# Expert outputs kept one row per choice, and the last two experts' rows brought to the tokens by one-hot matmuls

## The chip, the cores and the metric

The kernel runs on one core of one Trainium2 chip. The metric is the device time of one execution in microseconds (us), and the median of several runs is compared. The engines are named in the profile as PE (TensorE matmuls) with PEld (its weight loads), DVE (VectorE), ACT (ScalarE), POOL (GpSimd) and SP (SyncE, which issues most DMAs). A name with a q behind it (SPq, POOLq) is the engine's sequencer, which issues DMAs, waits and branches. Tiles are 128 partitions wide; S and D, the tokens and the model's width, are both 1024, so that a [1024, 1024] tensor in f32 has 4.19 MB.

## The reference

One decoder layer: attention of two kinds side by side, a cross-attention into memory tokens, a mixture of experts, a final RMS norm. The change touches the mixture's output and the norm:

```python
# each token: one group of experts, then the top 2 experts in it, with weights
weights = (g_gate * e_gate).reshape(-1)
expert_ids = (g_sel * EXPERTS_PER_GROUP + e_sel).reshape(-1)
...
def block_fn(args):
    tok, wt, e = args
    xb = h_pad[tok]
    hidden = jax.nn.silu(xb @ w_gate[e]) * (xb @ w_up[e])
    return (hidden @ w_down[e]) * wt[:, None].astype(hf.dtype)
...
out = jnp.zeros((n_tok + 1, d), hf.dtype).at[slot_token].add(y.reshape(n_slots, d))[:n_tok]
...
x = x + _hierarchical_moe(...)
return _rms_norm(x, norm_final_g)
```

There are 32 experts; 1024 tokens with two choices each make 2048 rows of expert output, 64 to an expert on average.

## The kernel before

Most of the kernel is written against a recorder, `Sched`. An engine call is recorded, and `flush` (line 337) puts all recorded operations into a static order by a greedy simulation with its own prices, then emits them to the engines' queues in that order. An operation recorded earlier has precedence among those that are ready. `hold` and `drop` keep a tile's buffer beyond its last recorded use. In the profile nearly all operations carry the helper's line, L523, so they are told apart by the names of their tiles. SBUF tiles of 4 KB a partition come from one pool of 50 buffers (`t4`, line 588).

Up to about 842 us the kernel computes attention, cross-attention and routing. For each 128 tokens `r_keep` (line 1476) writes the normed rows to XN and the residual rows to ACC, both in DRAM. `r_index` (1603) makes `sidx`, for each of 32 experts and 96 slots the number 2 x token + choice of the row in that slot (a large number where the slot is empty), and from it `gidx`, the token.

`experts` (1762) goes over the 32 experts. For expert e, `moe_load` asks for weights up to two experts ahead, as six buffers of 0.52 MB. `m_x` gathers the expert's tokens from XN with an indirect DMA on GpSimd, `m_split` splits each weight buffer into a high and a low part (ScalarE casts, VectorE subtracts), `m_gu` and `m_h` compute the hidden layer, and `m_d` (1746) the output: two PSUM banks of 512 columns, scaled by the routing weight on ScalarE into y, then an indirect DMA on GpSimd that adds the rows to ACC. Each scatter waits for the one before, as both touch ACC.

Behind the experts the recorded operations are flushed. Then stands a block (1880 to 1998) that a register decides: where an expert has over 96 rows, it works off the rest in a loop with its own weight loads on SP and scatters on GpSimd. In the profiled execution no instruction of the block's inside ran. The block's branch is line 1881.

The tail (2002 to 2018) is recorded anew: it loads the final gain and the eight tiles of ACC, and for groups of tiles (`TAIL`) squares them on ScalarE with a sum, takes the inverse root in a chain of twelve small VectorE operations, scales on VectorE and writes out.

Of the kernel before, what the change touches and what calls it, by code (L numbers as in the profile page):

```python
# [22 lines left out]
P = 128  # L23
# [32 lines left out]
WHOLE_GU = range(0)  # L56
WHOLE_D = range(4)
WHOLE_PV = ()
TAIL = ((0,), (1, 2), (3, 4), (5, 6, 7))
PARK = range(8)  # L60
NPRE = 0
NXG = 3
# [463 lines left out]
def f32(t):  # L526
    return t.bitcast(F32)
# [30 lines left out]
def hybrid_kernel(ctx: ExitStack, tc: tile.TileContext, a, out):  # L558
# [111 lines left out]
    VD = dram.tile([NT, P, 8 * P], F32, name="VD")  # L670
    VM = dram.tile([NT, P, 8 * P], F32, name="VM")
    XN = dram.tile([S, D], F32, name="XN")
    ACC = dram.tile([S, D], F32, name="ACC")

    def rsqrt(dst, v, tmp):

# [520 lines left out]
    w3 = keep.tile([P, 3, 2, NT], BF16, name="w3")  # L1197
    wsl = keep.tile([P, NE], F32, name="wsl")
    gidx = keep.tile([P, NE], I32, name="gidx")
    w_out, w_mq, w_mo, w_mkv = (a[n].rearrange("o d c -> (o d) c") for n in  # L1200
                                ("w_out", "w_mem_q", "w_mem_o", "w_mem_kv"))
    pr = sm
# [273 lines left out]
    def r_keep(t):  # L1476

        x = t4("xn")

        nc.gpsimd.tensor_mul(x.rearrange("p (k q) -> p q k", k=KT), *[  # L1480
            v.rearrange("p (q k) -> p q k", k=KT) for v in (xr[t], rt["gb"])])
        nc.scalar.activation(x, x, AF.Copy, scale=rs_[t])
        nc.sync.dma_start(XN[t * P:(t + 1) * P], x)
        nc.sync.dma_start(ACC[t * P:(t + 1) * P], xr[t])

    def r_factors(c, *sizes):

# [115 lines left out]
    def r_index():  # L1603

        tb = acc()[0:NS, 0:NE]
        n = 0
        for c in range(NCH):
            oh, vv = lane[c]
            for k in range(2):
                for t in range(TPC):  # L1610
                    for i in range(2):
                        mm(tb, oh[:, k, t], vv[:, k, t, i * NE:(i + 1) * NE], start=n == 0, stop=n == 31)
                        n += 1
        ti = rper(NE)[0:NS]
        sidx = rper(NE, dt=I32)
        with nc.chain():
            nc.vector.tensor_scalar(ti, tb, 0.0, 4096.0, op0=OP.is_equal, op1=OP.mult)
            nc.vector.scalar_tensor_tensor(sidx[0:NS], tb, -1.0, ti, op0=OP.add, op1=OP.add)
            nc.vector.tensor_scalar(gidx[0:NS], sidx[0:NS], 1, None, op0=OP.arith_shift_right)
# [35 lines left out]
        nc.vector.tensor_copy(nov, obend[:, NE - 1:NE])  # L1655


    w_g, w_u, w_d = (a[n].rearrange("o e d f -> (o e) d f") for n in ("w_expert_gate", "w_expert_up", "w_expert_down"))
    pieces = {}

# [73 lines left out]
    def m_h(e):  # L1734
        sg = st[e]["sg"]
        hp = bank()
        for k in range(2):
            nc.tensor.transpose(hp[:, k * NS:(k + 1) * NS], sg[0:NS, k * P:(k + 1) * P], ident[0:NS, 0:NS])
        if e in WHOLE_D:
            h = st[e]["h"] = t4("hw", P, 2, CH)  # L1740
            nc.scalar.copy(h[:, 0, 0:2 * NS], hp[:, 0:2 * NS])
        else:
            h = st[e]["h"] = two("hid")
            split((h[:, 0, 0:2 * NS], h[:, 1, 0:2 * NS]), hp[:, 0:2 * NS])

    def m_d(e):
        h = st[e]["h"]
        y = t4("y")
        for n in range(2):
            yp = bank()  # L1750
            for k in range(2):
                sl = slice(k * NS, (k + 1) * NS)
                if e in WHOLE_D:
                    mm(yp[0:NS], h[:, 0, sl], pieces[e, 4 + k][:, n], start=k == 0, stop=k == 1)
                else:
                    wh, wl = st[e][4 + k]
                    mm3(yp[0:NS], h[:, 0, sl], h[:, 1, sl], wh[:, n], wl[:, n], k == 0, k == 1)
            nc.scalar.activation(y[0:NS, n * 512:(n + 1) * 512], yp[0:NS], AF.Copy, scale=wsl[0:NS, e:e + 1])
        nc.gpsimd.indirect_dma_start(out=ACC[:, :], out_offset=Rows(ap=gidx[0:NS, e:e + 1], axis=0), in_=y[0:NS],
                                     in_offset=None, bounds_check=S - 1, oob_is_err=False, compute_op=OP.add)  # L1760

    def experts():
        for e in range(NE + 1):
            if e < NE:
                for i in range(AHEAD):
                    moe_load(e + i)
                m_x(e)
                for j in range(4):
                    m_split(e, j)
                moe_load(e + AHEAD)  # L1770
                if e > 0:
                    m_h(e - 1)
                m_gu(e)
                for j in range(4, 6):
                    m_split(e, j)
            if e > 0:
                if e == NE:
                    m_h(e - 1)
                m_d(e - 1)

# [30 lines left out]
    def place(units, *knots):  # L1811

        n = len(units)
        for i, u in enumerate(units):
            x = (i + 0.5) / n * (len(knots) - 1)
            j = int(x)
            line.append((knots[j] + (x - j) * (knots[j + 1] - knots[j]), u))

    place([c_angles, u_load_q, u_load_kv], *T["ul"])
    for c in range(NCH):  # L1820
        place(c_units(c), *T[f"cu{c}"])
        place(u_units(c), *T[f"uu{c}"])
# [48 lines left out]
    nc.flush()  # L1871
    lazy, nc = nc, tc.nc
    mm = nc.tensor.matmul
    A_, obst_, obend_, rank_, nov_, hc_, w3_, XN_, ACC_ = (v.real() for v in (A, obst, obend, rank, nov, hc, w3, XN, ACC))
    ident_, iota_ = hc_[:, 32:160], hc_[:, 160:288]

    def rbank():
# [3 lines left out]
    with tc.If(rnov > 0):  # L1881
# [71 lines left out]
        with tc.For_i(0, rnov, 1) as b:  # L1953
# [37 lines left out]
            for n in range(2):  # L1991
                yp = rbank()
                for k in range(2):
                    mm(yp, hT_[:, k * P:(k + 1) * P],
                       wdn[k][:, n * 512:(n + 1) * 512], start=k == 0, stop=k == 1)
                nc.vector.tensor_scalar(y[:, n * 512:(n + 1) * 512], yp, wx, None, op0=OP.mult)
            nc.gpsimd.indirect_dma_start(out=ACC_[:, :], out_offset=bass.IndirectOffsetOnAxis(ap=ix[:, 1:2], axis=0), in_=y,
                                         in_offset=None, bounds_check=S - 1, oob_is_err=False, compute_op=OP.add)
    nc = lazy


    gf = t4("gfin")
    nc.sync.dma_start(gf, a["norm_final_g"].partition_broadcast(P))
    y_t = ACC.rearrange("(t p) d -> t p d", p=P)
    o_t = out.rearrange("o (t p) d -> (o t) p d", p=P)
    ys = [t4("yt") for _ in range(NT)]
    for t in range(NT):
        nc.sync.dma_start(ys[t], y_t[t])

    for tiles in TAIL:  # L2010
        n = len(tiles)
        ss = carve("ss1")(3, n)
        for i, t in enumerate(tiles):
            nc.scalar.activation(t4("sq"), ys[t], AF.Square, accum_out=ss[:, 0, i:i + 1])
        rsqrt_mean(ss[:, 2], ss[:, 0], D, ss[:, 1])
        for i, t in enumerate(tiles):
            nc.vector.scalar_tensor_tensor(ys[t], ys[t], ss[:, 2, i:i + 1], gf, op0=OP.mult, op1=OP.mult)
            nc.sync.dma_start(o_t[t], ys[t])


_INS = ["x", "mem", "positions", "norm_mix_g", "w_in", "diff_lambda_q1", "diff_lambda_k1", "diff_lambda_q2",
# [21 lines left out]
```

## Time and profile before

| | us |
|---|---|
| median of 3 runs | 1226.58 |
| lowest and highest run | 1223.6, 1228.83 |
| the profiled execution | 1223.93 |
| its span, first to last instruction | 1222.1 |

The profile is of one execution on the core. Busy time over the span: PE 1099.2 us, DVE 875.7, ACT 801.0, POOL 422.5. Matmuls are pipelined and their ends modelled, so PE's busy time is not its time at its peak. The clock granted to TensorE was 0.95 of full speed in the mean. The DMA share is the mean busy share of the core's 16 DMA engines.

### The profile page before, as it was taken

The numbers are of one execution on the slowest core, as the hardware profiler recorded it, in microseconds if no ns is written. First come the engines' busy times: TensorE is split into PE (matmuls) and PEld (weight loads), VectorE is DVE, ScalarE is ACT, GpSimd is POOL, SyncE is SP. The second block draws the span as 40 slices with busy tenths as digits, with TensorE's granted clock in tenths as the row PEclk, the third lists the DMA queues.
The fourth block names the chain that finished last, engine by engine and source line by source line (L and its number), as shares of the span: only waits on it lengthen the run. The fifth ranks groups of instructions, "written<-read, shape, count | busy, mean of one in ns | idle before, by whom it ended". The sixth has DMA issues, their size and how long they took to land. (4 is left out here: it accounts for less than half of the span.)

```text
span 1222.1 us, 19622 instructions
## 1 busy us (share of the span) xinstructions
PE 1099.2 (90%) x6285; PEld 897.8 (73%) x6285; DVE 875.7 (72%) x2044; ACT 801.0 (66%) x1597; POOL 422.5 (35%) x378
## 2 busy tenths in 40 slices
PE   3999999998798999999999999994998999899970
PEld 3998898897666887678999888884665776666640
DVE  5946535468899879999482466776666898778855
ACT  5735327589988789987361455651676887778853
POOL 2214321258837456966121001153132322222120
PEclk9999999999899999899899999995998999999995
DMA  9118898459844553456441132877899999999967
GB/s 299 32 49 296 306 381 254 132 156 249 214 106 134 155 159 82 121 154 201 156 139 36 36 115 70 286 230 251 274 307 284 299 307 318 324 329 331 340 206 280
DMA packets 145115, 256.56 MB, mean 210 GB/s; under 512 B 17035, under 2 KB 65522, under 8 KB 145010
## 3 DMA queue, kind: packets, MB, share of 16 engines
q1 hardware_dynamic: 128960, 208.22, 53.7%
q0 software_dynamic: 15680, 46.75, 12.7%
q8 instruction: 50, 0.82, 0.3%
q14 instruction: 55, 0.45, 0.1%
q10 hardware_dynamic: 370, 0.32, 0.1%
HBM read 208.57 MB, written 55.05 MB: 216 GB/s over the span
## 5 line engine op out<-in xcount | busy, mean ns | idle before, releaser
L523 DVE TENSOR_TENSOR elo<-eraw,ehi 128x1024 fp32r<-128x1024 f32 x182 | 218.8, 1230 | 53.8 <-ACT ehi L523 48.2
L523 ACT CAST ehi<-eraw 128x1024 fp32r<-128x1024 f32 x184 | 189.5, 1054 | 23.1 <-DMA eraw<-in_w_expert_up_dram 16.8
L523 PE MATMUL bank<-ehi,xT 128*96 128x512 f32 x512 | 173.7, 411 | 5.7 <-ACT y L523 4.3
L523 PE MATMUL bank<-k,q 128*128 128x512 f32 (+5 forms) x480 | 129.7, 379 | 8.9 <-DMA k<-KD 1.8
L523 POOL DMA_INDIRECT ACC<-y,gidx x32 | 52.3, 1633 | 216.0 <-ACT y L523 183.6
L523 DVE TENSOR_TENSOR pT<-bank,pT 128x512 fp32r<-128x512 f32 (+2 forms) x208 | 109.0, 561 | 24.0 <-ACT pT L523 23.5
L523 PE MATMUL acc<-pT,v 128*128 128x512 f32 (+3 forms) x384 | 113.2, 376 | 10.0 <-ACT pT L523 5.1
L523 PEld LDWEIGHTS bank<-ehi,xT 128*96 128x96 f32 x512 | 85.6, 167 | 43.8 <-ACT y L523 9.4
L523 ACT CAST pT<-bank 128x512 fp32r<-128x512 f32 (+2 forms) x208 | 93.4, 497 | 28.6 <-PE bank L523 27.4
L523 PE MATMUL bank<-hc,pt 128*128 128x128 f32 x640 | 102.2, 291 | 7.9 <-POOL pt L523 6.0
L523 PE MATMUL bank<-elo,xT 128*96 128x512 f32 x256 | 104.4, 408 | 1.9 <-DVE elo L523 1.4
L523 PEld LDWEIGHTS bank<-k,q 128*128 128x128 f32 (+1 forms) x480 | 82.6, 196 | 26.6 <-DVE mx L523 7.1
L523 PE MATMUL lbank<-whi,mix 128*128 128x256 f32 x512 | 97.0, 286 | 0.0
L523 PEld LDWEIGHTS bank<-hc,pt 128*128 128x128 f32 x640 | 80.8, 150 | 20.1 <-POOL pt L523 7.8
L523 PE MATMUL lbank<-whi,hT 128*128 128x256 f32 (+1 forms) x384 | 86.8, 312 | 0.0
L523 PEld LDWEIGHTS acc<-pT,v 128*128 128x128 f32 x384 | 64.8, 193 | 27.2 <-ACT pT L523 11.0
L523 PEld LDWEIGHTS lbank<-whi,mix 128*128 128x128 f32 x512 | 81.4, 192 | 0.2
L523 PE MATMUL lbank<-hT,whi 128*128 128x512 f32 x256 | 81.1, 395 | 0.0
L523 PE MATMUL bank<-ehi,hid 128*96 128x512 f32 x224 | 75.6, 395 | 1.2 <-ACT hid L523 0.8
L523 PE MATMUL lbank<-wlo,mix 128*128 128x256 f32 x256 | 72.6, 284 | 0.0
L523 DVE TENSOR_REDUCE mx<-bank 128x1 f32<-128x512 f32 (+3 forms) x112 | 61.2, 571 | 14.7 <-PE bank L523 14.4
L523 POOL TENSOR_TENSOR O<-O,sh 64x512 f32<-64x512 f32 x32 | 41.5, 1298 | 79.1 <-ACT O L523 67.0
(623 smaller groups left out, 2671.9 us busy)
## 6 DMA issues: line engine op xcount, KB each, us to landing
eraw<-in_w_expert_gate_dram SPq DMA_DIRECT2D x128, 256.0 KB
eraw<-in_w_expert_up_dram SPq DMA_DIRECT2D x128, 256.0 KB
eraw<-in_w_expert_down_dram SPq DMA_DIRECT2D x64, 512.0 KB
k<-KD SPq DMA_DIRECT2D x72, 128.0 KB
QM<-st POOLq DMA_DIRECT2D x16, 512.0 KB, 6.8
q<-QM SPq DMA_DIRECT2D x16, 512.0 KB
wraw<-in_w_out_dram SPq DMA_DIRECT2D x16, 512.0 KB
wraw<-in_w_in_dram SPq DMA_DIRECT2D x12, 512.0 KB
```

Source lines behind the costliest of these rows:

```text
L523: getattr(getattr(self.nc, eng), name)(*[real(v) for v in a], **{n: real(v) for n, v in k.items()})
```

## The change

The DRAM tensor ACC goes. Two take its place: XR, with the residual rows, and Y, with 2048 rows, one for each token's each choice. `r_keep` writes XR where it wrote ACC. Y is cleared: one tile of zeros, and 16 writes of 128 rows from it on SP, placed among the units of attention (300 to 560 us of the plan). `sidx` moves into a longer-lived tile. `m_d` scatters to Y by `sidx`, without adding. For the last two experts (`NLAST`) it doesn't scatter: it splits the two halves of y into a high part (ScalarE) and a low part (VectorE) and keeps them.

`m_end` is recorded after expert 31's gate and up products and ahead of its down product: it loads the eight tiles of XR, the sixteen tiles of Y (a tile takes the first or second choices of 128 tokens) and the final gain, and for each of the last two experts makes a one-hot matrix (slot by token) of eight pieces with 18 small VectorE operations. These loads are flushed ahead of the overflow block. The block scatters to Y and ends with its own reload of the sixteen Y tiles.

In the tail a tile is XR's plus the two of Y, plus, for each half, a PSUM bank into which four one-hot matmuls (two experts, high and low) bring the last experts' rows. The first add of even tiles, and their product with the gain, are on GpSimd; even tiles are scaled on ScalarE.

```diff
-TAIL = ((0,), (1, 2), (3, 4), (5, 6, 7))
+NLAST = 2
+TAIL = ((0, 1), (2, 3), (4, 5), (6, 7))
+TAILV = (1, 3, 5, 7)
...
-    ACC = dram.tile([S, D], F32, name="ACC")
+    XR = dram.tile([S, D], F32, name="XR")
+    Y = dram.tile([2 * S, D], F32, name="Y")
...
+    sidx = sums.rearrange("p t h -> p (t h)")[:, 0:NE].bitcast(I32)
...
-        nc.sync.dma_start(ACC[t * P:(t + 1) * P], xr[t])
+        nc.sync.dma_start(XR[t * P:(t + 1) * P], xr[t])
...
+    y_t = Y.rearrange("(t p k) d -> t k p d", p=P, k=2)
...
-            nc.scalar.activation(y[0:NS, n * 512:(n + 1) * 512], yp[0:NS], AF.Copy, scale=wsl[0:NS, e:e + 1])
-        nc.gpsimd.indirect_dma_start(out=ACC[:, :], out_offset=Rows(ap=gidx[0:NS, e:e + 1], axis=0), in_=y[0:NS],
-                                     in_offset=None, bounds_check=S - 1, oob_is_err=False, compute_op=OP.add)
+            w = wsl[0:NS, e:e + 1]
+            if e >= NE - NLAST:
+                yl = last[e, n] = two("yl")
+                nc.scalar.activation(yl[0:NS, 0], yp[0:NS], AF.Copy, scale=w)
+                nc.vector.scalar_tensor_tensor(yl[0:NS, 1], yp[0:NS], w, f32(yl[0:NS, 0]), op0=OP.mult, op1=OP.subtract)
+                nc.hold(yl)
+            else:
+                nc.scalar.activation(y[0:NS, n * 512:(n + 1) * 512], yp[0:NS], AF.Copy, scale=w)
+        if e >= NE - NLAST:
+            return
+        nc.gpsimd.indirect_dma_start(out=Y[:, :], out_offset=Rows(ap=sidx[0:NS, e:e + 1], axis=0), in_=y[0:NS],
+                                     in_offset=None, bounds_check=2 * S - 1, oob_is_err=False)
...
+    def y_zero():
+
+        z = t4("zero")
+        nc.gpsimd.memset(z, 0.0)
+        return [lambda i=i: nc.sync.dma_start(Y[i * P:(i + 1) * P], z) for i in range(2 * NT)]
+
+    def m_end():
+
+        for t in range(NT):
+            ys.append([t4("yt")])
+            nc.sync.dma_start(ys[t][0], XR[t * P:(t + 1) * P])
+        for t in range(NT):
+            for k in range(2):
+                ys[t].append(t4("yt"))
+                nc.sync.dma_start(ys[t][1 + k], y_t[t, k])
+            nc.hold(*ys[t])
+        for e in range(NE - NLAST, NE):
+            g = sm.tile([P, 1 + NT], F32, name="lastg", bufs=2)
+            nc.vector.tensor_copy(g[0:NS, 0:1], gidx[0:NS, e:e + 1])
+            oh = last[e] = t4("oh", P, NT, P, dt=F32R)
+            for t in range(NT):
+                nc.vector.tensor_scalar(g[0:NS, 1 + t:2 + t], g[0:NS, 0:1], -float(t * P), None, op0=OP.add)
+                nc.vector.tensor_scalar(oh[0:NS, t], iota_f[0:NS], g[0:NS, 1 + t:2 + t], None, op0=OP.is_equal)
+            nc.hold(oh)
+        last["gf"] = t4("gfin")
+        nc.sync.dma_start(last["gf"], a["norm_final_g"].partition_broadcast(P))
+        nc.hold(last["gf"])
...
             if e > 0:
                 if e == NE:
+                    m_end()
                     m_h(e - 1)
                 m_d(e - 1)
...
+    place(y_zero(), 300, 560)
...
+        y_t_ = Y_.rearrange("(t p k) d -> t k p d", p=P, k=2)
+        for t in range(NT):
+            for k in range(2):
+                nc.sync.dma_start(ys[t][1 + k].real(), y_t_[t, k])
     nc = lazy
...
         for i, t in enumerate(tiles):
-            nc.scalar.activation(t4("sq"), ys[t], AF.Square, accum_out=ss[:, 0, i:i + 1])
+            z, y0, y1 = ys[t]
+            (nc.vector if t in TAILV else nc.gpsimd).tensor_add(z, z, y0)
+            nc.vector.tensor_add(z, z, y1)
+            for b in range(2):
+                po = bank()
+                m = [(last[e][0:NS, t], last[e, b][0:NS, x]) for e in range(NE - NLAST, NE) for x in range(2)]
+                for x, (l, r) in enumerate(m):
+                    mm(po, l, r, start=x == 0, stop=x == len(m) - 1)
+                v = z[:, b * 512:(b + 1) * 512]
+                nc.vector.tensor_add(v, po, v)
+            nc.scalar.activation(y0, z, AF.Square, accum_out=ss[:, 0, i:i + 1])
         rsqrt_mean(ss[:, 2], ss[:, 0], D, ss[:, 1])
         for i, t in enumerate(tiles):
-            nc.vector.scalar_tensor_tensor(ys[t], ys[t], ss[:, 2, i:i + 1], gf, op0=OP.mult, op1=OP.mult)
-            nc.sync.dma_start(o_t[t], ys[t])
+            z = ys[t][0]
+            if t in TAILV:
+                nc.vector.scalar_tensor_tensor(z, z, ss[:, 2, i:i + 1], gf, op0=OP.mult, op1=OP.mult)
+            else:
+                nc.scalar.activation(z, z, AF.Copy, scale=ss[:, 2, i:i + 1])
+                nc.gpsimd.tensor_mul(z, z, gf)
+            nc.sync.dma_start(o_t[t], z)
```

## Rows read from the trace of the kernel before

**Rows 1.** Windows by stage: busy us (instructions) by engine, PEclk, DMA share, GB/s.
```profile
430.00:560.00 130.00, 122.67 (x698) 98.48 (x696) 117.72 (x342) 114.70 (x258) 87.61 (x53) 0.93 0.53 143
842.00:938.00 96.00, 83.82 (x404) 57.31 (x404) 56.87 (x69) 58.50 (x88) 26.88 (x23) 0.90 0.89 271
938.00:1024.00 86.00, 85.22 (x418) 60.40 (x417) 76.96 (x91) 74.54 (x108) 24.41 (x19) 1.00 0.99 306
1024.00:1114.00 90.00, 80.87 (x366) 54.56 (x364) 68.48 (x80) 68.44 (x96) 21.95 (x16) 0.94 1.00 329
1114.00:1176.00 62.00, 58.56 (x260) 38.37 (x259) 53.02 (x61) 52.70 (x74) 11.80 (x7) 1.00 0.99 337
1176.00:1194.00 18.00, 8.69 (x37) 5.44 (x35) 4.36 (x5) 5.58 (x9) 2.83 (x2) 0.87 0.35 71
```
**Rows 2.** Chain of waits near the end: start us, us, what.
```profile
1182.62 5.49 DMA ACC<-y,gidx
...
1188.86 5.22 DMA ACC<-y,gidx
```
**Rows 3.** Timeline, last y and last tail group: start, us, engine, operation, [idle before].
```profile
1185.64 0.69 ACT L523 ACTIVATE y<-bank,wsl 96x512 f32<-96x512 f32 x1 [0.68 <-PE bank L523]
...
1211.84 0.57 DVE L523 TENSOR_SCALAR ss<-ss 128x3 f32<-128x3 f32 x3
...
1214.22 3.68 DVE L523 SCALAR_TENSOR_TENSOR yt<-yt,ss,gfin 128x1024 f32<-128x1024 f32 x3
```
**Rows 4.** DMA queues, 850 to 1175 us: packets, MB, share; scatters, median us to land.
```profile
q1 hardware_dynamic: 38821, 84.76, 76.3%
q0 software_dynamic: 6505, 15.33, 20.0%
...
ACC<-y,gidx POOLq DMA_INDIRECT x30, 8.2
```
**Rows 5.** Groups of instructions, 850 to 1175 us: the gathers, busy us, mean ns.
```profile
L523 POOL DMA_INDIRECT xg<-XN,gidx x29 | 31.7, 1092 | 43.5 <-PE bank L523 37.1 <-issue 6.4
```
**Rows 6.** DMA queues, 840 to 870 us, GpSimd's queue with gathers alone.
```profile
q0 software_dynamic: 784, 1.89, 22.9%
...
xg<-XN,gidx POOLq DMA_INDIRECT x7, 5.9
```
**Rows 7.** DMA queues, 871 to 880 us, GpSimd's queue with one scatter.
```profile
q0 software_dynamic: 112, 0.23, 13.3%
```
**Rows 8.** The overflow block's branch on SP: duration ns, first and last start; its waits.
```profile
L1881 SPq EVENT_SEMAPHORE  x9: 17/17/17, 1170.7 to 1177.7; - x9
...
SPq L1881 <- SPq L1881: 7.3, 7, 1.9
```
**Rows 9.** Window in which the tail's loads and first writes run, columns as rows 1.
```profile
1195.50:1206.00 10.50, 0.00 (x0) 0.00 (x0) 6.36 (x27) 7.00 (x13) 0.00 (x0) 0.50 1.01 371
```
**Rows 10.** Timeline of SP's DMA issues, from the last weight pieces on.
```profile
1168.30 0.98 SPq L523 DMA_DIRECT2D eraw<-in_w_expert_down_dram  x2
1177.82 0.35 SPq L523 DMA_DIRECT2D gfin<-in_norm_final_g_dram  x1
```
**Rows 11.** Groups of VectorE by shape, whole span: busy us, mean ns, idle before.
```profile
L523 DVE TENSOR_TENSOR elo<-eraw,ehi 128x1024 fp32r<-128x1024 f32 x182 | 218.8, 1230 | 53.8 <-ACT ehi L523 48.2 <-issue 2.3 <-DMA eraw<-in_w_expert_gate_dram 1.7
L523 DVE TENSOR_TENSOR xr<-lbank,xr 128x512 f32<-128x512 f32 x16 | 11.0, 688 | 12.0 <-PE lbank L523 11.9
L523 DVE SCALAR_TENSOR_TENSOR yt<-yt,ss,gfin 128x1024 f32<-128x1024 f32 x8 | 9.9, 1282 | 0.1
```
**Rows 12.** Groups of GpSimd by shape: a product of two tiles in SBUF.
```profile
L523 POOL TENSOR_TENSOR xn<-xr,gb 128x1024 f32<-128x1024 f32 x8 | 19.3, 2414 | 53.2 <-DVE xr L523 44.4 <-ACT xn L523 5.7 <-issue 3.1
```
**Rows 13.** Timeline of GpSimd and VectorE around 833 us.
```profile
832.75 2.38 POOL L523 TENSOR_TENSOR elo<-eraw,ehi 128x1024 fp32r<-128x1024 f32 x1
833.40 1.74 DVE L523 TENSOR_TENSOR rtmp<-rtmp 128x4 f32<-128x4 f32 x1
```
**Rows 14.** DMA queues, 1183.5 to 1188.5 us, GpSimd's queue with one scatter alone.
```profile
q0 software_dynamic: 112, 0.29, 40.2%
```

More of the change, by code (lines that the diff above doesn't have):

```diff
@@ L1614, in r_index @@
         ti = rper(NE)[0:NS]
-        sidx = rper(NE, dt=I32)
         with nc.chain():
@@ L1747, in m_d @@
         h = st[e]["h"]
-        y = t4("y")
+        y = t4("y") if e < NE - NLAST else None
         for n in range(2):
@@ L1757, in m_d @@
                     mm3(yp[0:NS], h[:, 0, sl], h[:, 1, sl], wh[:, n], wl[:, n], k == 0, k == 1)
-            nc.scalar.activation(y[0:NS, n * 512:(n + 1) * 512], yp[0:NS], AF.Copy, scale=wsl[0:NS, e:e + 1])
-        nc.gpsimd.indirect_dma_start(out=ACC[:, :], out_offset=Rows(ap=gidx[0:NS, e:e + 1], axis=0), in_=y[0:NS],
-                                     in_offset=None, bounds_check=S - 1, oob_is_err=False, compute_op=OP.add)
+            w = wsl[0:NS, e:e + 1]
[10 more added lines that the diff above has]
+                                     in_offset=None, bounds_check=2 * S - 1, oob_is_err=False)
+    ys = []
+    last = {}
+    def y_zero():
[22 more added lines that the diff above has]
+        nc.hold(last["gf"])
     def experts():
@@ L1873, in hybrid_kernel @@
     mm = nc.tensor.matmul
-    A_, obst_, obend_, rank_, nov_, hc_, w3_, XN_, ACC_ = (v.real() for v in (A, obst, obend, rank, nov, hc, w3, XN, ACC))
+    A_, obst_, obend_, rank_, nov_, hc_, w3_, XN_, Y_ = (v.real() for v in (A, obst, obend, rank, nov, hc, w3, XN, Y))
     ident_, iota_ = hc_[:, 32:160], hc_[:, 160:288]
@@ L1996, in hybrid_kernel @@
                 nc.vector.tensor_scalar(y[:, n * 512:(n + 1) * 512], yp, wx, None, op0=OP.mult)
-            nc.gpsimd.indirect_dma_start(out=ACC_[:, :], out_offset=bass.IndirectOffsetOnAxis(ap=ix[:, 1:2], axis=0), in_=y,
-                                         in_offset=None, bounds_check=S - 1, oob_is_err=False, compute_op=OP.add)
+            nc.gpsimd.indirect_dma_start(out=Y_[:, :], out_offset=bass.IndirectOffsetOnAxis(ap=ix[:, 0:1], axis=0), in_=y,
+                                         in_offset=None, bounds_check=2 * S - 1, oob_is_err=False)
+        y_t_ = Y_.rearrange("(t p k) d -> t k p d", p=P, k=2)
+        for t in range(NT):
+            for k in range(2):
+                nc.sync.dma_start(ys[t][1 + k].real(), y_t_[t, k])
     nc = lazy
-    gf = t4("gfin")
-    nc.sync.dma_start(gf, a["norm_final_g"].partition_broadcast(P))
-    y_t = ACC.rearrange("(t p) d -> t p d", p=P)
+    mm = nc.tensor.matmul
+    gf = last["gf"]
     o_t = out.rearrange("o (t p) d -> (o t) p d", p=P)
-    ys = [t4("yt") for _ in range(NT)]
-    for t in range(NT):
-        nc.sync.dma_start(ys[t], y_t[t])
     for tiles in TAIL:
@@ L2013, in hybrid_kernel @@
         for i, t in enumerate(tiles):
-            nc.scalar.activation(t4("sq"), ys[t], AF.Square, accum_out=ss[:, 0, i:i + 1])
+            z, y0, y1 = ys[t]
[9 more added lines that the diff above has]
+            nc.scalar.activation(y0, z, AF.Square, accum_out=ss[:, 0, i:i + 1])
         rsqrt_mean(ss[:, 2], ss[:, 0], D, ss[:, 1])
         for i, t in enumerate(tiles):
-            nc.vector.scalar_tensor_tensor(ys[t], ys[t], ss[:, 2, i:i + 1], gf, op0=OP.mult, op1=OP.mult)
-            nc.sync.dma_start(o_t[t], ys[t])
+            z = ys[t][0]
[5 more added lines that the diff above has]
+            nc.sync.dma_start(o_t[t], z)
+    nc.drop(gf, *[v for y in ys for v in y], *[v for k, v in last.items() if k != "gf"])
 _INS = ["x", "mem", "positions", "norm_mix_g", "w_in", "diff_lambda_q1", "diff_lambda_k1", "diff_lambda_q2",
```

## The prediction

> **What bounds the kernel now.** I read first the table by stage [rows 1]. Through the expert stage (842 to 1176 us) the 16 DMA engines are full (0.89, then 0.99 to 1.00), TensorE is nearly so: 85.2 of 86 us up to 1024, then 80.9 of 90 and 58.6 of 62. So weights set the pace there, and TensorE would take over after a gain of at most its idle time, 12.2 + 0.8 + 9.1 + 3.4 = 25.5 us. From 1176 on nothing is full: the stretch to 1194 has DMA at 0.35 and TensorE at 8.7 of 18 us. The chain of waits shows what that stretch is: two accumulating scatters, one behind the other, 5.5 and 5.2 us, the second held until the first has landed [rows 2]. The last y rows are out of PSUM at 1185.64 + 0.69 = 1186.3 [rows 3], and the span ends at 1222.1: 35.8 us of tail, with VectorE's chains and scalings as its last part.
>
> **Part 1: scatters without accumulation.** Between 850 and 1175 us the queue of GpSimd's DMAs takes 20.0% of the engines, 65.0 us, for 30 scatters [rows 4] and 29 gathers [rows 5]. Gathers alone cost 22.9% of 30 us / 7 = 0.98 us each [rows 6]. That leaves (65.0 - 28.5) / 30 = 1.22 us for a scatter; a stretch with a single scatter gives 13.3% of 9 us = 1.20 [rows 7]. A plain scatter isn't in the trace. Its nearest rows: the gather of the same rows, 0.98, and the weights, 76.3% of 325 us for 84.8 MB = 2.93 us per MB [rows 4], which for a scatter's 0.26 MB is 0.77. I take the middle, 0.87: 0.35 x 30 = 11 us less DMA work before the last weights. Ends: 0 (a plain row costs what an added one does) and 0.45 x 30 = 14; dearer than with the read I exclude. As the engines are full, this moves the last weights, which land at about 1177.7 (the end of SP's waits, [rows 8]), to 1166.7, and the last y to 1175.3; the second half of the split of y on VectorE adds 0.69, so VectorE is free for the tail at 1176.
>
> **Part 2: what must be loaded now.** Before, 4.19 MB of ACC; now 4.19 MB of XR, 8.39 MB of Y and 0.52 MB of gain: 25 loads of 0.52 MB. They stand on SP behind all weights. With loads of this kind the engines moved 371 GB/s, 1.41 us for one [rows 9]. XR fills 1166.7 to 1178. Y waits for the scatter of expert 29, one expert ahead of the one in the chain at 1182.62 [rows 2]; even at that one's time, 11 us earlier and 5.5 us to land, it is there at 1177, so XR hides this wait. All 25 have landed at 1166.7 + 25 x 1.41 = 1202. Here a page gives another price: the Trainium skill, "SBUF — State Buffer", in its summary of rules for kernel authors, says to estimate transfers between HBM and SBUF at about 358 GB/s; the trace has 371, and by the page the loads would land 1.3 us later.
>
> **Part 3: a wait that the change adds.** The loads stand ahead of the block for overflowing experts, and the tail behind it. Before, SP doesn't enter that block. Skipping it costs SP nine semaphore instructions, from 1170.7 to 1177.7, of which seven wait, 7.3 us in all [rows 8], though SP issued the last two weight pieces from 1168.30 on; the very next DMA behind the block, the gain, goes out at 1177.82, right after the last wait [rows 10]. I read this so: the block holds SP loads, and SP, skipping it, may stand in for their landing counts only once its own earlier loads have landed. Before, this cost nothing, as SP then had to wait for the scatters until 1188.86 + 5.22 = 1194 [rows 2]. Now the block reloads Y into the very tiles that the tail adds, so the adds must wait for the counts that SP sets. Queued behind it on SP are only the out DMAs; who waits is VectorE, from 1176. The last eight of the 25 loads land from 1192 to 1202. The block issues ten weight loads first, which goes once round the eight counts and two further, so the first tile needs about the third of the last eight: 1166.7 + 20 x 1.41 = 1195. Ends: 1192 (the first) and 1202 (all).
>
> **Part 4: the tail on VectorE.** Prices from [rows 11]: 12 adds of 128x1024 at 1.23 = 14.8; 16 adds from PSUM of 128x512 at 0.69 = 11.0; 4 scalings at 1.28 = 5.1; 4 rsqrt chains at 1214.22 - 1211.84 = 2.38 [rows 3], 9.5. Sum 40.4 us, against 8 scalings and 4 chains before, 19.8. GpSimd has 4 adds at about 2.4 [rows 12] and 4 products, 2.4 or a little less: 18 us. These aren't free: at 833.40 a VectorE operation on four elements of SBUF takes 1.74 us, to the end of GpSimd's operation of 832.75 + 2.38 [rows 13]. So VectorE's work with two SBUF inputs (14.8 + 5.1 and some 7 of the chains, 27) and GpSimd's 18 can't lie beside each other, 45 us; adds from PSUM may lie beside GpSimd. Ends 40.4 (no collision) and 58 (all collide). I take 45, as the kernel's own plan keeps the two apart where it can. ScalarE's squares and scalings and TensorE's 64 one-hot matmuls run beside it: at 8.69 / 37 = 0.23 us each [rows 1], twice that at half clock, 30 us; were VectorE not the bound, 30 would be theirs. After the last scaling, which ended at 1217.9, the last rows took 4.2 us to leave; this stays.
>
> **Part 5: small things.** 34 small VectorE operations for the one-hots go into its idle time ahead of the tail (53 of 62 us busy before 1176, then a wait for Y); uncovered some 6 us at about 0.17 each. The 16 clearing writes stand on SP among the loads of attention, where DMA is at 0.53 and TensorE at 122.7 of 130 us [rows 1]: nothing, with 16 x 1.41 = 23 us as the worst, if every one held a load that TensorE needs; a gain is excluded. One buffer of 50 for the zeros: nothing to 3 us.
>
> **The sum.** 1195 + 45 + 4.2 = 1244, against a span of 1222.1: 22 us more. The profiled execution took 1223.93 (1.8 us around its span), so 1246; the median of the three runs is 2.65 above it, 1226.58. I take 1247. Own range: weights +11 to -3, start -3 to +7, VectorE -5 to +13, not all at once: 1236 to 1262.
>
> **Rivals.**
> A, no gate: the tail's adds wait for their own loads only. For it: SP's waits concern SP, and no row shows another engine held by them. Against: the block writes the same tiles. The first tile then starts after 10 loads, 1180.8; + 45 + 4.2 = 1230, or 1225 with 40.4. That is 1228 to 1235 with what lies around the span.
> B, faster: accumulation is dearer than the share says. Two scatters alone show it: one of them keeps the engines busy for 40.2% of 5 us = 2.0 us [rows 14], and (2.0 - 0.77) x 30 = 37 us is more than TensorE lets through, so up to 25 us come back. Without the gate and without collisions the end is 1177.7 - s + 14.1 + 40.4 + 4.2 = 1236.4 - s: at s = 25 it is 1211, so 1216. It decides from s = 20 on; with the gate it would need over 34. Against: in the full stage the share gives 1.22.
> C, the clearing writes hold the loads of attention: 10 us on top of the sum, 1257.
>
> **How the numbers follow.** The forecast 0.58, A 0.18, B 0.17, C 0.07. Range 1216 to 1262: it takes in A and the edge of B, and leaves out half of B and the upper ends of the forecast and C. What a measurement of this kernel can tell from no change is about 0.5%, 6 us: 1220.4 to 1232.7. A lies about that upper edge, so half of it and a little of the forecast's lower end count as the same. Faster 0.16, same 0.14, slower 0.70.
>
> **What would show it.** In the profile after: 1.0 us or less of DMA share per scatter, and the last weights 8 to 14 us earlier; SP's semaphore instructions at the block ending with the last Y load, 25 to 30 us after the last weights, and VectorE's first tail add behind one of them, after idling 15 us or more; then a VectorE busy 40 us with its adds at times stretched to the end of a GpSimd operation. Wrong if the first tail add comes within 15 us of the last weights (A), if the weights come over 20 us earlier (B), or if attention ends later than before by more than 5 us (C).

## The result, and the profile after

The changed kernel takes 1258.23 us (median of 4 runs, 1252.56 to 1261.89), the kernel before, beside it on the same chip, 1227.7 us. The ratio is 1.0236, with a 95% interval from 1.0211 to 1.0261: 2.4% slower. The prediction was 1247, range 1216 to 1262. The profiled execution took 1255.23 us, its span is 1253.0.

The windows by stage of the kernel after answer to [rows 1]; columns as there. The last two stretches are its tail, which before was part of the stretch from 1186 to 1222.

```profile
842.00:938.00 96.00, 83.18 (x422) 57.81 (x423) 61.44 (x116) 54.95 (x82) 25.41 (x23) 0.87 0.85 270
938.00:1024.00 86.00, 85.27 (x418) 60.47 (x417) 75.38 (x89) 74.63 (x109) 22.08 (x18) 1.00 0.99 336
1024.00:1114.00 90.00, 86.55 (x418) 59.79 (x417) 76.76 (x90) 75.47 (x110) 20.28 (x17) 1.00 1.00 339
1114.00:1166.00 52.00, 51.31 (x235) 34.81 (x234) 48.03 (x60) 47.44 (x67) 7.17 (x6) 1.00 1.02 375
1166.00:1194.00 28.00, 17.47 (x67) 11.83 (x65) 9.47 (x22) 4.50 (x8) 0.00 (x0) 0.89 1.03 408
1194.00:1222.00 28.00, 13.12 (x32) 9.43 (x32) 24.39 (x34) 6.91 (x11) 14.53 (x5) 0.56 0.20 79
1222.00:1253.00 31.00, 0.49 (x2) 0.00 (x0) 19.77 (x47) 6.89 (x9) 8.24 (x3) 0.50 0.25 101
```

The expert stage is denser: 1024 to 1114 us holds 86.55 us of TensorE's work where it held 80.87, and the DMA engines move 339 GB/s where they moved 329. What was won there ends in the stretch from 1166 to 1194: DMA is full with the tail's loads and VectorE works 9.47 of 28 us. Then come 59 us of tail with DMA at 0.20 and 0.25.

GpSimd's timeline puts the marks. First two of the kernel before, its first gather and the scatter of expert 29; then, of the kernel after, the first gather, the scatter of expert 29 (the last one now), the first and second addition of the tail, and the last product.

```profile
842.31 1.08 POOL L523 DMA_INDIRECT xg<-XN,gidx  x1 [0.91 <-DVE gidx L523]
...
1173.71 1.69 POOL L523 DMA_INDIRECT ACC<-y,gidx  x1 [7.68 <-ACT y L523]
```
```profile
848.44 1.08 POOL L525 DMA_INDIRECT xg<-XN,gidx  x1 [0.91 <-DVE lastg L525]
...
1163.16 1.18 POOL L525 DMA_INDIRECT Y<-y,sums  x1 [7.90 <-ACT y L525]
1194.77 2.33 POOL L525 TENSOR_TENSOR yt<-yt 128x1024 f32<-128x1024 f32 x1 [30.43 <-DMA yt<-Y]
1199.80 8.99 POOL L525 TENSOR_TENSOR yt<-yt 128x1024 f32<-128x1024 f32 x3 [2.69 <-SPq L1929]
...
1244.19 2.34 POOL L525 TENSOR_TENSOR yt<-yt,gfin 128x1024 f32<-128x1024 f32 x1 [7.35 <-ACT yt L525]
```

With them the 30.9 us between the spans (1253.0 against 1222.1) can be laid out. The first gather went from 842.31 to 848.44: +6.1 in the front. From there to the scatter of expert 29 (1173.71 before, [rows 2] show the next one): 331.4 before, 314.7 after, -16.7. From that scatter to the end: 48.4 before, 89.8 after, +41.4. The 89.8 are 31.6 until the first addition and 58.2 of tail.

Why the first addition comes at 1194.77 is on SP. Its DMA issues, then its instructions at the branch of the overflow block (form as in [rows 8]), and its wait there:

```profile
1158.16 1.01 SPq L525 DMA_DIRECT2D eraw<-in_w_expert_down_dram  x2
1160.27 6.41 SPq L525 DMA_DIRECT2D yt<-XR  x8
1168.40 0.33 SPq L525 DMA_DIRECT2D gfin<-in_norm_final_g_dram  x1
1170.79 20.30 SPq L525 DMA_DIRECT2D yt<-Y  x16
1213.67 33.22 SPq L525 DMA_DIRECT2D out_dram<-yt  x8
```
```profile
L1929 SPq EVENT_SEMAPHORE  x9: 17/17/17, 1192.5 to 1200.9; - x9
```
```profile
SPq L1929 <- SPq L1929: 8.5, 8, 1.3
```

The nine semaphore instructions lasted from 1170.7 to 1177.7 before; now they begin behind the last Y load, at 1192.5, and go on to 1200.9 as those loads land. The second addition names the branch as its releaser. The first names a DMA of Y instead; that not the loads but the branch holds it until 1194.77 is shown by the experiment without the reload below.

VectorE's timeline from the last rows on: its last work of the experts, and then the tail's first operations.

```profile
1180.17 0.75 DVE L525 SCALAR_TENSOR_TENSOR yl<-bank,wsl,yl 96x512 fp32r<-96x512 f32 x1 [0.64 <-ACTq L1929]
1197.14 2.36 DVE L525 TENSOR_TENSOR yt<-yt 128x1024 f32<-128x1024 f32 x2 [16.21 <-POOL yt L525]
1199.41 1.28 DVE L525 TENSOR_TENSOR yt<-bank,yt 128x512 f32<-128x512 f32 x2
1200.61 5.93 DVE L525 TENSOR_TENSOR yt<-yt 128x1024 f32<-128x1024 f32 x2
```

16 us idle, and then two additions that take 5.93 us instead of 2.4, beside GpSimd's. Later in the tail the two engines can be seen to take turns; first GpSimd's product of one tile, then VectorE's scaling and the two additions behind it:

```profile
1212.63 3.21 POOL L525 TENSOR_TENSOR yt<-yt,gfin 128x1024 f32<-128x1024 f32 x1 [3.85 <-ACT yt L525]
```
```profile
1212.36 1.28 DVE L525 SCALAR_TENSOR_TENSOR yt<-yt,ss,gfin 128x1024 f32<-128x1024 f32 x1
1213.56 4.50 DVE L525 TENSOR_TENSOR yt<-yt 128x1024 f32<-128x1024 f32 x2
```

The scaling ends at 1213.64, and GpSimd's product, 2.34 us in the last group, ends 2.20 us after that, at 1215.84. VectorE's two additions, started at 1213.56, end at 1218.06, 2.22 us after GpSimd's end, which is about what two take alone.

The clearing writes don't go out among the loads of attention. SP's issue in the kernel before, and then its issues in the kernel after:

```profile
17.11 1.68 SPq L523 DMA_DIRECT2D wraw<-in_w_in_dram  x2
```
```profile
17.78 19.69 SPq L525 DMA_DIRECT2D Y<-zero  x16
38.39 1.64 SPq L525 DMA_DIRECT2D wraw<-in_w_in_dram  x2
```

The zeros need no input, so the planner puts the writes at 17.8 us, and two loads of the input projection's weights behind them went from 17.11 to 38.39.

### The profile page after: what moved, and what is told of

Same layout as the page of the kernel before. It is cut to its first block, busy times and chain, and to the rows that moved or that the text cites. A ratio compares the mean times of both kernels' runs of the same rounds, so it can differ in the third digit from the quotient of the medians.

```text
span 1253.0 us, 19902 instructions
## 1 busy us (share of the span) xinstructions
PE 1112.4 (89%) x6349; PEld 911.4 (73%) x6349; DVE 911.8 (73%) x2115; ACT 801.5 (64%) x1601; POOL 428.0 (34%) x376
## 5 line engine op out<-in xcount | busy, mean ns | idle before, releaser
L525 PE MATMUL bank<-ehi,xT 128*96 128x512 f32 x512 | 170.3, 404 | 2.2 <-ACT y L525 0.7
L525 PE MATMUL bank<-k,q 128*128 128x512 f32 (+5 forms) x480 | 129.1, 378 | 10.1 <-ACT O L525 2.5
L525 DVE TENSOR_TENSOR pT<-bank,pT 128x512 fp32r<-128x512 f32 (+3 forms) x208 | 108.2, 560 | 18.4 <-ACT pT L525 17.9
L525 ACT CAST pT<-bank 128x512 fp32r<-128x512 f32 (+3 forms) x208 | 91.9, 496 | 25.8 <-PE bank L525 25.1
L525 POOL DMA_INDIRECT Y<-y,sums x30 | 35.1, 1171 | 196.0 <-ACT y L525 177.8
L525 PEld LDWEIGHTS lbank<-whi,hT 128*128 128x128 f32 x384 | 67.0, 195 | 6.6 <-DVE hT L525 5.9
```

The costliest lines, as they stand in the source:

```text
L525: getattr(getattr(self.nc, eng), name)(*[real(v) for v in a], **{n: real(v) for n, v in k.items()})
```

## The experiments

Each runs beside the kernel before on the same chip; ratios are to that. The profile of the kernel before is from another chip, on which its median was up to 4 us lower than in some of these comparisons, so small differences of marks against it show little: in four kernels that have the change's clearing writes and expert stage (the changed one, without the reload, without GpSimd, loads behind the block), the first gather lies anywhere from 848.44 to 850.70.

**Plain scatters alone.** The kernel before, with

```diff
-    in_offset=None, bounds_check=S - 1, oob_is_err=False, compute_op=OP.add)
+    in_offset=None, bounds_check=S - 1, oob_is_err=False)
```

> The kernel before with one edit: the experts' scatters write to ACC without adding (so the residual and the first of a token's two expert rows are lost from the output; nothing else is left out). Theory: the gain inside the expert stage is the price of the addition, 0.6 us of DMA per scatter instead of 1.2. Then the 30 scatters ahead of the last weights give back some 16 to 18 us, the last weights land near 1161 instead of 1177.7, the start of the stage stays at 842 and the tail behind the last y keeps its length (35.8 us, perhaps 2 to 4 less, as two plain scatters land sooner): 1205 to 1211 us, ratio 0.983 to 0.987. Rival: the stage after is shorter because the planner's order changed and because two scatters are gone; then this kernel stays within 5 us of the kernel before.

Measured: 1203.95 us, ratio 0.980 (0.9761 to 0.9839), somewhat more than expected. GpSimd's last scatters, and the DMA queues from 850 to 1160 us (columns as [rows 4]):

```profile
1156.35 1.18 POOL L523 DMA_INDIRECT ACC<-y,gidx  x1 [7.84 <-ACT y L523]
...
1169.95 0.91 POOL L523 DMA_INDIRECT ACC<-y,gidx  x1 [4.16 <-DMA ACC<-y,gidx]
```
```profile
q1 hardware_dynamic: 38887, 84.98, 80.2%
q0 software_dynamic: 6621, 15.54, 15.2%
```

Expert 29's scatter comes 17.4 us earlier (1173.71 to 1156.35, with the first gather at 842.65 against 842.31), the span is 20.4 us shorter than that of the profile before; the other 3 us lie behind that scatter. By the working of Part 1 the queue's share now gives (0.152 x 310 - 29 x 0.98) / 30 = 0.62 us for a scatter. In the changed kernel a stretch of 9 us with one scatter, 877 to 886, says the same: 6.7% of 9 = 0.60, where [rows 7] had 13.3%.

```profile
q0 software_dynamic: 112, 0.23, 6.7%
```

So accumulation cost 0.6 us per scatter in the full stage, 17 to 18 us in all, and the stage gives all of it back. The rival, that the gain came from the planner's order and the two scatters fewer, is out: neither differs here.

**Without the reload in the block.** The changed kernel, with the block's loads of Y taken out:

```diff
-        for t in range(NT):
-            for k in range(2):
-                nc.sync.dma_start(ys[t][1 + k].real(), y_t_[t, k])
```

> The changed kernel without the reload of Y's sixteen tiles inside the overflow block (left out is that reload, which runs only if an expert overflows). Gate theory: the tail's adds no longer wait for the counts that SP sets behind the block, only for their own loads; the first tail add comes at about 1182 instead of 1194.8 (VectorE is free at 1181, the first Y tiles land at about 1181), and the rest of the tail moves with it as VectorE sets it: 1241 to 1246 us, 10 to 14 less than the changed kernel. Rival: the adds were waiting for the data itself (25 loads at 1.4 us), not for SP; then the first add stays within 3 us of 1195 and the time within 4 us of the changed kernel.

Measured: 1243.94 us, ratio 1.0118 (1.0082 to 1.0155), span 1238.5. GpSimd's timeline, the first addition and a later one:

```profile
1178.96 2.38 POOL L525 TENSOR_TENSOR yt<-yt 128x1024 f32<-128x1024 f32 x1 [15.98 <-DMA yt<-Y]
...
1195.30 2.78 POOL L525 TENSOR_TENSOR yt<-yt 128x1024 f32<-128x1024 f32 x1 [2.75 <-SPq L1929]
```

The first addition comes 15.8 us earlier and the span is 14.5 us shorter, while SP waits at the branch as before (8.6 us in 8 waits against 8.5). So SP's waiting is not what costs; what costs is that the tail's tiles hang on it, and the reload makes them. Only one later addition still names the branch.

**Late clearing writes.** The changed kernel, with the zeros made from a value of attention and each write held behind the one before:

```diff
-        z = t4("zero")
-        nc.gpsimd.memset(z, 0.0)
...
+            if i == 0:
+                z.append(t4("zero"))
+                nc.vector.tensor_scalar(z[0], f32(VC[0]).rearrange("p a c -> p (a c)"), 0.0, None, op0=OP.mult)
+            else:
+                nc.gpsimd.memset(z[0][:, 0:1], 0.0)
...
-    place(y_zero(), 300, 560)
+    place(y_zero(), 420, 680)
```

> The changed kernel with Y cleared later: the zeros are made from a tile of the cross-attention's keys (times zero) instead of by a memset, and each next write waits for the one before, so the sixteen writes fall behind some 380 us instead of 17 to 37 us. Theory: the early writes held the loads of w_in on SP's queue by 21 us and TensorE's matmuls by 5.5 us at half clock behind that, and so all that follows by 6 us; without it the first gather comes at 842 to 843 instead of 848.4 and the time is 5 to 8 us less than the changed kernel's. Rival: the 6 us come from the planner's other order in attention or from the buffer that the zeros hold; then the first gather stays at 847 or later. If the writes hurt attention where they now stand, the stretch from 380 to 560 us grows and the gain is less.

Measured: 1244.4 us, ratio 1.012 (1.0076 to 1.0164), span 1242.1, the tail again 58.2 us. The first gather comes at 837.50: 10.9 us ahead of the changed kernel's, and 4.8 ahead of the kernel before's, more than undoing the delay would give. SP issues the writes from 452.6 to 578.1 us, later than the 380 that was expected. Window 50 to 64 us, of the kernel before, of the changed kernel and of this one:

```profile
50.00:64.00 14.00, 14.00 (x71) 12.95 (x70) 13.52 (x43) 8.68 (x29) 5.58 (x13) 1.00 0.10 39
```
```profile
50.00:64.00 14.00, 8.46 (x32) 7.87 (x31) 11.91 (x44) 6.97 (x21) 0.98 (x3) 0.76 0.17 65
```
```profile
50.00:64.00 14.00, 14.00 (x71) 12.97 (x71) 13.52 (x44) 8.60 (x29) 5.57 (x13) 1.00 0.10 39
```

With the early writes TensorE is busy for 8.46 of 14 us here, at a mean granted clock of 0.76 (between its two levels, 1.2 and 2.4 GHz), against 14.00 at 1.00. It stands idle for 5.5 us up to 56.27, by the profile for VectorE's hT; the chain from the late loads to that wait was not followed further.

**The clearing writes by themselves.** As the 4.8 us were in nobody's expectation, the writes were put alone into the kernel before, in either place (Y is written and read by nobody).

> The kernel before with nothing added but the buffer Y, its zeroed tile and the 16 clearing writes in the place that the change gives them (Y is read by nobody). If the clearing writes by themselves delay the front, as the changed kernel's first gather at 848.44 instead of 842.31 suggests: first gather at 847 to 850, span 1227 to 1230, ratio 1.004 to 1.007. Rival, that the delay came from another part of the change (the order that the planner finds with it): first gather within 2 us of 842.31, ratio 0.998 to 1.002.

> The kernel before with the same 16 clearing writes, but among the loads of attention, as in e3_late_clear (the zeros are made from a value that exists only then, and each write waits for the one before it). In e3_late_clear the first gather came at 837.50, 4.8 us ahead of the kernel before. If the writes cost nothing there and the 4.8 us were an accident of the planner's order in that kernel: first gather at 841 to 844, ratio 0.998 to 1.002. If the late writes themselves bring the other order: first gather at 836 to 839, ratio 0.994 to 0.998. If they hold loads of attention, as the prediction's case C has it: first gather at 845 or later, ratio over 1.002.

Measured: early, 1234.05 us, ratio 1.0034 (1.0018 to 1.0051); late, 1224.68 us, ratio 0.9939 (0.9915 to 0.9963). The first gather of the early one, and of the late one:

```profile
850.65 1.07 POOL L523 DMA_INDIRECT xg<-XN,gidx  x1 [0.92 <-DVE gidx L523]
```
```profile
840.44 1.08 POOL L523 DMA_INDIRECT xg<-XN,gidx  x1 [0.91 <-DVE gidx L523]
```

So early writes delay the front by themselves: TensorE's window 50 to 64 again has 8.41 us (14.00 with late ones). In time that is 4 us here, less than the 8 us by which the gather is late against the profile of before; gather, span (1231.9) and ratio all lie just outside what was expected, the ratio on the small side. The late ones show no cost: the ratio is 0.6% better than with no writes at all, though nobody reads what they write, and the medians of the two places lie 9.4 us apart. The first gather at 840.44 lies between the two ranges of the expectation, the ratio next to that for another order of the planner. On this chip the spans with late writes are 1218.8 to 1223.7 (4 runs), without writes 1224.0 to 1233.4 (17 runs), so the gain is there; that it comes from when the planner issues the neighbours of the writes is likely but not shown. What follows is a caution: 0.6% can come from an edit that does no useful work.

**The tail without GpSimd.** The changed kernel, with VectorE doing GpSimd's four additions and four products too:

```diff
-TAILV = (1, 3, 5, 7)
+TAILV = range(8)
```

> The changed kernel with all tiles of the tail on VectorE: 16 adds of 128x1024 and 8 scalings there, none on GpSimd, and no scaling on ScalarE. Theory of the shared port: GpSimd's 8 operations in the tail give VectorE nothing, as its adds and scalings with two inputs in SBUF wait until they end. VectorE then works 16 x 1.22 + 16 x 0.62 + 4 x 2.4 + 8 x 1.28 = 49 us without stretching from about 1195, against 47 stretched plus the 2.3 before and the 2.3 behind it: the tail is 1 to 5 us shorter and the time within -6 to 0 us of the changed kernel. Rival: GpSimd's work lay beside VectorE's; then VectorE's 4 more adds and 4 more scalings come on top and it is 7 to 10 us slower.

Measured: 1253.12 us, ratio 1.0183 (1.0145 to 1.0221), span 1252.8. Its expert stage ended 4.7 us later (the scatter of expert 29 at 1167.82), so its tail is what counts: from its first addition at 1199.20 it takes 53.6 us against 58.2, with eight operations of 1.2 us more on VectorE. Of the 4.6 us, 2.3 lie ahead of the last operation's end (49.5 us against 51.8) and 2.4 behind it (4.1 against 6.5). VectorE's first addition here, and its groups by shape from 1193 to 1253 us, first of the changed kernel, then of this one:

```profile
1199.20 1.23 DVE L525 TENSOR_TENSOR yt<-yt 128x1024 f32<-128x1024 f32 x1 [15.17 <-SPq L1929]
```
```profile
L525 DVE TENSOR_TENSOR yt<-yt 128x1024 f32<-128x1024 f32 x12 | 22.5, 1903 | 16.2 <-POOL yt L525 16.2
```
```profile
L525 DVE TENSOR_TENSOR yt<-yt 128x1024 f32<-128x1024 f32 x16 | 18.9, 1221 | 16.5 <-SPq L1929 16.5
```

Sixteen additions in 18.9 us where twelve took 22.5: beside GpSimd one takes 1.90 us in the mean, alone 1.22. And with GpSimd gone, VectorE itself is what waits 16.5 us for SP's branch.

**Loads behind the block.** The changed kernel, with the tail's loads recorded behind the overflow block and no reload in it:

```diff
-            nc.sync.dma_start(ys[t][0], XR[t * P:(t + 1) * P])
...
-                nc.sync.dma_start(ys[t][1 + k], y_t[t, k])
...
     gf = last["gf"]
+    for t in range(NT):
+        ys.append([t4("yt") for _ in range(3)])
+        for v, src in zip(ys[t], (XR[t * P:(t + 1) * P], y_t[t, 0], y_t[t, 1])):
+            nc.sync.dma_start(v, src)
```

> Only the place of the loads is changed: the changed kernel with the 24 loads of XR and Y recorded behind the block for overflowing experts, tile by tile (XR, Y, Y), and without the block's reload of Y. Gate theory: SP's wait at the block then covers the weights alone and is over by about 1166, and the Y loads wait only for the scatters; three of them land 4 us later, so the first tail add starts as soon as the last rows are there, about 1181 instead of 1194.8, the span falls by 12 to 15 us from 1253.0 to 1238 to 1241, the ratio to the kernel before is 1.009 to 1.014. Rival, that the tail is held by the loads themselves or by the scatter of expert 29: SP's wait ends early, yet the first add stays at 1190 or later, the span over 1248.

Measured: 1245.31 us, ratio 1.0128 (1.0073 to 1.0184), as expected, but a span of 1245.3 and a first addition at 1188.12, between the 1181 expected and the rival's 1190; the span is 4 us over what was expected. SP's branch and issues:

```profile
L1921 SPq EVENT_SEMAPHORE  x9: 17/17/17, 1165.2 to 1171.7; - x9
```
```profile
1161.42 1.00 SPq L525 DMA_DIRECT2D eraw<-in_w_expert_down_dram  x2
1163.50 0.33 SPq L525 DMA_DIRECT2D gfin<-in_norm_final_g_dram  x1
1171.87 5.19 SPq L525 DMA_DIRECT2D yt<-XR  x8
1177.16 20.91 SPq L525 DMA_DIRECT2D yt<-Y  x16
```

The branch's waits now cover the weights alone and are over at 1171.7, 29 us sooner: the wait follows the loads recorded ahead of it, as Part 3 read it. But the loads then begin at 1171.87, not at 1160.27, and the planner issues all eight XR ahead of the first Y. The last weights were also 3.3 us later. Counted from expert 29's scatter (at 1170.26) the end is 75.0 us away instead of 89.8, about as without the reload (76.7).

**Additions on TensorE.** The kernel of the last experiment with the late writes, all scalings on VectorE, and each Y row added by an identity matmul into the bank of the one-hot matmuls (this last part is shown):

```diff
-            (nc.vector if t in TAILV else nc.gpsimd).tensor_add(z, z, y0)
-            nc.vector.tensor_add(z, z, y1)
...
+                m = [(ident, y[:, b * 512:(b + 1) * 512]) for y in (y0, y1)] + m
```

> The kernel of e5_loads_behind with the late clearing writes of e3_late_clear, and a tail in which the two loaded Y rows of a tile are added on TensorE: an identity matmul of each into the PSUM bank that the one-hot matmuls sum in, so the additions of 128x1024 on VectorE and all of GpSimd's part go. Theory (the tail is as long as VectorE's work with two SBUF inputs and GpSimd's together): what is left on VectorE is 16 adds from PSUM at 0.69, 8 scalings at 1.28 and 4 chains at 2.4, 31 us, from about 1170 on (the last rows some 11 us earlier, as in e3_late_clear), and 4 to 6 us to leave: span 1204 to 1211, 16 us and more below the kernel before, ratio 0.983 to 0.992. TensorE has 32 matmuls of 0.4 to 0.8 us and 64 of 0.24 beside it, 28 to 41 us: if it is the bound, the span is 1212 to 1220. Rival, that the tail is bound by the 24 loads and the exit and not by VectorE and GpSimd: a tail of 53 us or more, as in e4_no_gpsimd, the span over 1222.

Measured: 1230.3 us, ratio 1.0008 (0.9988 to 1.0029), span 1231.9; 12 us above even the expectation for TensorE as the bound (1212 to 1220). Groups of TensorE from 1170 us on:

```profile
L525 PE MATMUL bank<-yt,hc 128*128 128x512 f32 x64 | 32.0, 623 | 7.5 <-DMA yt<-Y 7.5
L525 PE MATMUL bank<-yl,oh 96*128 96x512 f32 x64 | 24.8, 511 | 0.0
```

An addition of 512 columns shows as two matmul records, 64 instead of the 32 reckoned with. A bank of eight records takes 2.65 us (VectorE's additions from PSUM start at 1181.13, 1183.77, 1186.42, 1189.08), 42 us for 16 banks: 1 us above the upper end of what was reckoned, 41. But TensorE begins at 1176.04 and not at 1170, after 7.5 us of waiting for the first Y behind eight XR, and behind that idle time its first bank takes 5.1 us, at a mean granted clock of 0.57 (1176.0 to 1181.2, near 1.2 GHz, the lower of its two levels), where later ones have 1.00 (2.4 GHz). So its work ends at 1221, and the span 10.9 us after that. The rival's marks, a span over 1222 and a tail of 53 us or more (55.9 from TensorE's start), are met too, so the span alone doesn't decide. The idle time does: once started, TensorE waits for nothing, and VectorE waits for TensorE's banks. The loads set the start, TensorE the pace.

**Split additions and another order of loads.** As the last, but in four tiles VectorE adds one of the two rows, and the XR loads of tiles 3 to 7 are held behind the first Y:

```diff
+TAILA = (1, 3, 5, 7)
...
+        if t > 2:
+            nc.gpsimd.tensor_copy(ys[t][0][:, 0:1], ys[t - 3][0][:, 0:1])
...
+            if t in TAILA:
+                nc.vector.tensor_add(z, z, y0)
...
+                m = [(ident, y[:, b * 512:(b + 1) * 512]) for y in ((y1,) if t in TAILA else (y0, y1))] + m
```

> The kernel of e6_pe_adds, whose tail TensorE set (16 banks of 8 matmul records, 2.65 us each, from 1176.0 to 1222), with two edits: in tiles 1, 3, 5 and 7 one of the two Y rows is added by VectorE again (4 x 1.23 us) and only the other by TensorE, and the XR loads of tiles 3 to 7 are held back behind the first Y loads, so that the first tile's Y has landed when the last rows are there, about 1170 and not 1176. TensorE: 8 banks at 2.65 and 8 at 2.0, 37 us; VectorE 11.0 + 4.9 + 10.2 + 9.6 = 36 us; both from 1170 on, 4 us for the last chain and product behind TensorE's last matmul and 4.2 us to leave, 7 for the two in turn at the start: span 1216 to 1224 against 1222.1 of the kernel before, ratio 0.989 to 0.997. If the loads and not TensorE set the start and the pace of e6_pe_adds, the second edit gives nothing and the first little: ratio 0.997 to 1.001.

Measured: 1222.16 us, ratio 0.993 (0.9907 to 0.9952), span 1215.8: the ratio is within what was expected, the span 0.2 us under it, and of the kernels here that compute the whole reference this has the lowest ratio. As both edits were made at once, what each gives is not shown. SP's loads:

```profile
1152.78 1.29 SPq L526 DMA_DIRECT2D yt<-XR  x3
1154.25 9.09 SPq L526 DMA_DIRECT2D yt<-Y  x10
1164.35 2.87 SPq L526 DMA_DIRECT2D yt<-XR  x3
```

TensorE starts the tail at 1163.87, 0.6 us after the last rows are there (1162.55 + 0.75 on VectorE), and a bank with one addition takes 1.80 us (1170.94 to 1172.74) where one with two takes 2.65: 0.85 us for one addition of 512 columns on TensorE. From expert 29's scatter (1149.88) the end is 65.9 us away, against 75.3 in the experiment before and 48.4 in the kernel before. But the kernel before with useless late writes has 0.9939 (0.9915 to 0.9963), which can't be told from this one's: of the 0.7%, nothing is shown to come from the change's idea.

## Why the prediction was right, and where its steps were off

The sign, the range and the main mechanism were right; the time lay 11 us above the forecast, and the tail began where it was forecast only because two errors of some 6 us cancelled. Step by step:

**Part 1, the scatters: mis-sized.** 1.22 us for an accumulating one stood; the plain one was put at 0.87, no lower than 0.77, and measures 0.60 to 0.62. So 17 us were saved, not 11, and the limit of 14 was too narrow. What failed was the lower bound: it took 0.26 MB for a scatter where [rows 7] show 0.23, and priced the bytes like the weights' (2.93 us per MB), while 0.23 MB in 0.60 us is 2.6, in a stretch where the queues' shares add up to over 100%. Rival B was right that accumulation is dearer than taken, but it needed over 34 us with the gate.

**The last weights: right by luck.** The forecast was 11 us earlier, SP issued the last pieces 10.1 us earlier (1168.30 to 1158.16). That is 17 us of scatters less 6 us of a later front, neither of which was forecast at that size.

**Part 2, the loads: near.** All landed at 1202 by the forecast, by SP's last wait about 1201. From 1166 to 1194 us, filled almost wholly by these loads, DMA moved 408 GB/s; the trace of before had shown 371. By the 358 GB/s that the Trainium skill, "SBUF — State Buffer", in its summary of rules for kernel authors, gives for estimating transfers, they would have landed later than forecast; the measurement decides.

**Part 3, the gate: right.** The forecast was a first addition at 1195 that waits for SP at the skipped block; it came at 1194.77, and without the reload at 1178.96. Rival A, in which no engine is held by SP's waits, is out: the same loads let the first addition start 15.8 us sooner when only the reload is gone, and in the kernel without GpSimd VectorE waits 16.5 us for SP's branch. The finer reading, that the first tile needs the third of the last eight counts, fits (nine steps from 1192.5 to 1200.9 put the third at 1194.6) but was not tested by itself.

**Part 4, the tail: mis-sized by 9 us.** Forecast 45 and 4.2 to leave, 49.2; measured 58.2. VectorE's own stretch, 1197.14 to 1244.19, is 47.0 us, 2.0 over the 45. The collision was right in kind and somewhat small: 4.6 us were taken for it above the 40.4 without, and the stretched additions cost 22.5 - 12 x 1.22 = 7.9 us. Left out was that the two engines are also in series: GpSimd does the first addition before VectorE can begin (2.4 us) and the last product after it has ended (2.3). And 6.5 us from GpSimd's last product to the end stand where 4.2 were taken. Together that is 2.0 + 2.4 + 2.3 + 2.3 = 9.0. The Trainium skill, "SBUF — State Buffer", section "Who interferes with whom", calls the ports that VectorE and GpSimd share an exclusive lock, not a throttle; the trace agrees, in the stretch from 1212.36 to 1218.06 above, where each engine finishes about one plain duration after the other's end. And the tail is shorter with all of it on VectorE.

**Part 5, the clearing writes: wrong in place.** They were taken at nothing since they were thought to lie among attention's loads, as their due time says. SP issues them at 17.8 us, where two loads of the input projection's weights wait behind them: 6.1 us at the first gather, 4 us of time when alone. So a mark that the prediction named for being wrong, a front over 5 us later, was met. Case C had the cost, but in attention; the late writes of the experiments, which do lie there, show none. That the zeros depend on nothing, and so can go out at once, could have been read in the diff. The one-hots show no cost: they are 34 operations, 17 for each expert (not the 18 given with the change); 16 of them lie at 1165.3 to 1169.6, and VectorE idles 16.2 us ahead of the tail. The other 18 run at 847.6 to 848.8, just behind the token indices, and the first gather follows those indices at the same distance as before (0.88 us).

**The sum.** 1195 + 45 + 4.2 = 1244 was forecast, 1194.8 + 58.2 = 1253.0 came. All of the span's miss lies in the tail; the start was met because the cheaper scatters and the later front, each some 6 us, cancelled. The other 2 us of the 11 lie between the span and the median: 5.2 where 3 were taken.

## What to carry to other kernels

Before moving loads ahead of a conditional block, look whether the block writes the tiles that they fill: skipping it can cost the engine that loads a wait for all that it has in flight, and everyone who reads those tiles a wait for that engine. An addition taken off the path by DMA comes back as loads and additions elsewhere: count where it lands (here 17 us saved ahead of the scatter of expert 29 and 41 added behind it, some 15 of them by the wait at the block), and don't spread elementwise work on large SBUF tiles over VectorE and GpSimd without pricing it as one queue. Where a planner orders the queues, as here, writes that depend on nothing may go out first and stand ahead of what the start needs; give them something to wait for, and look in the trace where they went.

## What the runs showed of the hardware

An indirect scatter of 0.23 MB in rows of 4 KB takes 0.60 to 0.62 us of the 16 DMA engines' time plain and 1.20 to 1.22 us accumulating in a full stage, a factor of two; a gather, which here moves 0.27 MB (1.89 MB for seven, [rows 6]), had 0.98.

In this kernel SP's wait at the skipped block follows the loads recorded ahead of it: 1192.5 to 1200.9 us with the tail's loads there, 1165.2 to 1171.7 with weights alone.

On VectorE an addition of 128x1024 with both inputs in SBUF and an operation of GpSimd on such tiles took turns: 1.22 us alone, 1.90 us in the mean beside GpSimd.

The kernels that end behind GpSimd took 2.3 us longer to end than those that end behind VectorE. From the last operation to the end of the span: 6.5 us in the changed kernel (1244.19 + 2.34 to 1253.0), 6.5 without the reload and with the loads behind the block, against 4.2 in the kernel before, 4.1 without GpSimd and 4.1 with the additions on TensorE. It isn't the output: the DMA engines have moved the last of it 4.3 us before the end in the changed kernel and 1.9 us before it in the kernel before. SP's longest wait for PE's sequencer in the end of the program is 2.6 us against 0.5. What lies behind that wasn't tried and stays open.
